# Shift columns, context-first attention units and a joined last phase in a two-block fp32 kernel

## The chip, the core and the metric

One core of one Trainium2 chip runs the whole program. The metric is the device time of one execution in microseconds (us); shown are medians of several runs. The engines are TensorE (PE, with its weight loads apart as PEld), VectorE (DVE), ScalarE (ACT), GpSimd (POOL) and SyncE (SP), which issues the DMAs. TensorE's clock has two levels, 2.4 and 1.2 GHz; the profile gives the granted one as a share, so 1.00 is the first and 0.50 the second.

## What is computed

Two blocks over 512 tokens of 1024 channels, all in fp32:

```
first block, twice (l = 0, 1), mod = ada(c):
  h += 0.5*gate * swiglu(norm(h)*(1+scale) + shift)      # FFN, d_ff 2816
  h += gate * mixer(modulate(norm(h)))                   # sparse attention + gated MLP
  h += 0.5*gate * swiglu(modulate(norm(h)))              # FFN
h = norm(h)*final_g
second block (latents h, 256 context tokens ctx):
  layer 0: h, ctx += gate * norm(pool_mixer(modulate(norm(.))))
           h, ctx += gate * norm(sq_relu_mlp(modulate(norm(.))))   # d_ff 4096
  layer 1: q, k, v = qkv of modulate(norm(h)) and modulate(norm(ctx)); norm, rope
           h += gate * norm(attend(q, k_all, v_all) @ w_o)
           h += gate * norm(sq_relu_mlp(modulate(norm(h))))
```

## The kernel before

Channels lie on partitions, tokens along the free axis. Each fp32 operand is split into a high and a low part, and each product is three matmuls of 512 columns (`mm3`, lines 114 to 116: weight-high by data-high, weight-high by data-low, weight-low by data-high). Weights come as 512 KB chunks on SP's queue into `raw`; ACT writes the high part (L98), DVE or POOL the low one (L100). A framework orders the instructions of each engine by its own model of readiness, with program order as priority, and places the semaphores; a step written later can so be issued earlier, except where an order is kept by hand (the transposes).

The stages, in us of the profiled execution: FFN (0,0) 0 to 410; mixer 0 to 840; FFN (0,1) to 1205; FFN (1,0) to 1560; mixer 1 to 1985; FFN (1,1) to 2355; the pooled mixer and the first MLP, with the context's MLP woven in, to 2920; QKV to 3075; attention to 3184; `w_o` to 3228; the last MLP to 3628.

**The start of a stage.** `Pre` (L237) lets a stage's first products begin before the normalisation of its input is known: `chunk` (L252) scales a finished chunk of h by the gain into `r`, the first products run on `r` (L284, L298, L324, L358), and the token factor and the shift are put in afterwards (`take`, L394). The shift then needs one column per product, weights times shift vector: `shift_products` (L209 to L223) is eight POOL instructions on one weight chunk, and a 128x1 matmul sums them (L310). Where the columns were made ahead, `shift_steps` (L225) did it in the filler of an earlier FFN: a DMA of the 512 KB chunk into `adaw`, the eight POOL instructions, the matmul L233 and a copy. `issue` (L305) starts a stage with its first two products side by side and, if no columns were made ahead, has POOL work and column matmuls in it; `first_two`, `both` and `last_two` do the same with another grouping, and `slow` puts the squares' sums (L150) on DVE where the first four are otherwise on POOL. Before the change the mixers and the first MLP had their columns ahead; FFNs (0,1), (1,0), (1,1) and the last MLP had not.

**The filler.** `ffn` (L495) draws steps of a generator between its product units; a pair such as (3, 2) gives the steps per unit. The steps compute the modulation vectors on DVE (L423, 1024 elements by a row, with an accumulator read behind it). What is left is drained at L554.

**The first MLP** (L1356 to L1460). After `pre.normed`, h is multiplied by `b1s`, eight DVE instructions (L1448, L1449); only then the main loop begins, in which `weave` mixes steps of the MLP (`mlp_steps`, L1319) with steps of the context's MLP at the rates of `WEAVE` (L38). The first four hidden products' results lie in PSUM until `take` (L401, `px`) has read them; the context's products (`nc`) want a PSUM bank too.

**QKV** (L1467 to L1633). Units 0 to 3 are queries, 4 keys, 5 values; each has two weight chunks, and 4 and 5 take two context tiles beside the four latent ones. `tok_proj` (L1555) does a unit's products (L1567 to L1569, 256 columns), its low weight parts on POOL; `heads` (L1572) norms and rotates on ACT and DVE into tiles `hx` of a pool of seven; `transposed` (L1606) is TensorE transposes (L1616) and a split. The loop at L1622 runs the units in the order 0, 1, 4, 2, 3, 5, with the transposes of a unit after the products of the next. Units 0 and 1 start from products made earlier (`first_tiles`).

**w_o and the last MLP** (L1675 to L1714) are two scopes with their own pools: `w_o`'s eight products, its norm, the residual (L1107, L1108) with `Pre.chunk`; then `issue` and the MLP.

Of the kernel before, what the change touches and what calls it, by code (L numbers as in the profile page):

```python
# [19 lines left out]
S = 512  # L20
# [17 lines left out]
WEAVE = (2, 3, 3, 1.65, 3)  # L38
# [13 lines left out]
def build(tc, d, stop=99):  # L52
# [412 lines left out]

    class Phase:
# [28 lines left out]
    def ffn(l, s, mods, fill, pre, tail, nf=(2, 2), start=None):  # L495

        with ExitStack() as st:
# [7 lines left out]
            def wsrc(n):  # L505
                return d["ffn_in"][l, s, n // 2, :, (n % 2) * 1024:(n % 2) * 1024 + 1024]
# [547 lines left out]
    for l in range(L):  # L1054
# [14 lines left out]
        box, tail = pre_tail(modsB, norm_g(l, 2))  # L1069
# [233 lines left out]
    def mlp_src(i, q):  # L1303
# [5 lines left out]
        ada2(p, 1, [ml1, mc1]), ctx_steps(ph), shift_steps(p, ml[:, 24:32], [mlp_src(0, q) for q in range(4)], mlp_cols)),  # L1309
        pre, ft, (3, 3))  # L1310
# [45 lines left out]
    with ExitStack() as st:  # L1356
# [74 lines left out]
        b1s = ph.hid_p.tile([128, S], F32, name="b1s", tag="hid0")  # L1431
# [18 lines left out]
        if stop <= 7:  # L1450
            st.close()
            nst.close()
            return finish_debug()

        ry = Rms(S, tmp)
# [11 lines left out]
    with ExitStack() as st:  # L1467
# [3 lines left out]
        with ExitStack() as ist:  # L1471
# [67 lines left out]
            bcl = bcast(r, S)  # L1539
            nh = [[rtile() for _ in range(2)] for _ in range(8)]  # L1540
            nhi, nlo = (lambda k: nh[k][0]), (lambda k: nh[k][1])
            modulate(h, bcl, gs, sh, S, tmp, nhi, nlo)
# [12 lines left out]
            def tok_proj(src, ctx):  # L1555

                tiles = ([(nch, ncl, 0), (nch, ncl, 1)] if ctx else []) + [(nhi, nlo, i) for i in range(4)]
                pss = [psum() for _ in range(len(tiles) // 2)]
                for k4 in range(2):
                    hi, lo = wget(src[:, k4 * 1024:(k4 + 1) * 1024], eng=G)  # L1560
                    for kk in range(4):
                        k = k4 * 4 + kk
                        w0, w1 = hi[:, kk * 256:(kk + 1) * 256], lo[:, kk * 256:(kk + 1) * 256]
                        for t, (xh, xl, i) in enumerate(tiles):
                            sl = slice(i * 128, (i + 1) * 128)
                            o = pss[t // 2][:, (t % 2) * 256:(t % 2) * 256 + 256]
                            T.matmul(o, xh(k)[:, sl], w0, start=k == 0 and t % 2 == 0, stop=False)  # L1567
                            T.matmul(o, xh(k)[:, sl], w1, start=False, stop=False)
# [278 lines left out]
```

## Time and profile before

| what | value |
|---|---|
| time, median of 3 runs | 3621.99 us (3616.54 to 3625.24) |
| the profiled execution's own time | 3629.45 us |
| its span in the profile | 3627.7 us |
| granted clock, mean | 0.979 |
| PE busy / PEld busy | 3472.6 us (96%) / 2861.7 us (79%) |
| DVE / ACT / POOL busy | 2299.2 (63%) / 1462.9 (40%) / 476.0 us (13%) |
| HBM read and written | 458.63 MB, 126 GB/s over the span |

The profiled execution lies 7.46 us above the median. Busy shares are means over stages that differ: in FFN (1,0) DVE is busy 259.1 of 355 us, in the last MLP with its start 190.3 of 399.7. What an edit in one stage is worth is read from the idle times of PE in that stage and from the granted clock there. A wait is put down to the one that ended last; square brackets at a line's end give the engine's idle time before it and what released it.

### The profile page before, as it was taken

How to read it: one execution, taken by the hardware profiler on the slowest of the kernel's cores; microseconds unless marked ns; L12 is line 12 of the kernel's file. 1: busy time of each engine (PE TensorE's matmuls, PEld its weight loads, DVE VectorE, ACT ScalarE, POOL GpSimd, SP SyncE). 2: the span in 40 equal slices, each digit the busy share in tenths (PEclk: the TensorE clock that was granted, in tenths of full speed). 3: DMA queues.
4: the chain of work that ended last, by engine and by line, in shares of the span. 5: the costliest groups of instructions: out<-in, count | busy, mean ns of one | idle time of the engine just before them, and what ended most of it. 6: DMA issues, size and time to landing. Idle time of an engine off the chain costs nothing.

```text
span 3627.7 us, 44600 instructions
## 1 busy us (share of the span) xinstructions
PE 3472.6 (96%) x16924; PEld 2861.7 (79%) x16924; DVE 2299.2 (63%) x3715; ACT 1462.9 (40%) x2487; POOL 476.0 (13%) x470
## 2 busy tenths in 40 slices
PE   7999999999999999999999999979999988989998
PEld 5788886788878888887688888868888877767886
DVE  8863677458753996378636966675445578654434
ACT  4222475433223422257624224654433435634232
POOL 4020113021000303022104020210000021130000
PEclk9999999999999999999999999989999999999999
DMA  6862221236862475231123763314444421013332
GB/s 237 287 235 92 95 77 48 69 103 240 292 210 91 156 244 171 88 109 51 44 88 133 248 234 99 108 56 134 128 130 127 133 66 59 1 47 99 97 96 70
DMA packets 140985, 461.55 MB, mean 127 GB/s; under 512 B 16869, under 2 KB 19297, under 8 KB 140641
## 3 DMA queue, kind: packets, MB, share of 16 engines
q1 hardware_dynamic: 140768, 458.69, 38.9%
q8 instruction: 133, 2.18, 0.2%
q14 instruction: 84, 0.68, 0.1%
HBM read 456.53 MB, written 2.10 MB: 126 GB/s over the span
## 4 chain that ended last, share of the span: by engine, by line
PE 63%; DVE 7%; ACT 2%; issue 1%; POOL 1%; DMA 1%; SPq 0%; DVEq 0%; ACTq 0%; POOLq 0%
PE mm L114 18%; PE mm L116 18%; PE mm L115 18%; DVE nt L200 1%; DVE wlo L100 1%; PE mm L324 1%; PE aux L1665 1%; PE aux L886 1%; DVE h L1108 0%; DVE n L206 0%; PE o L854 0%; ACT whi L98 0%; DVE ssum L150 0%; POOL shp L215 0%; PE o L115 0%
## 5 line engine op out<-in xcount | busy, mean ns | idle before, releaser
L98 ACT ACTIVATE whi<-raw 128x1024 fp32r<-128x1024 f32 (+2 forms) x636 | 619.3, 976 | 1469.1 <-PE mm L115 1075.0
L100 DVE TENSOR_TENSOR wlo<-raw,whi 128x1024 fp32r<-128x1024 f32 (+3 forms) x605 | 694.7, 1150 | 506.9 <-ACT whi L98 499.0
L114 PE MATMUL mm<-n,whi 128*128 128x512 f32 x2096 | 831.5, 397 | 14.2 <-ACT nt L202 9.2
L116 PE MATMUL mm<-n,wlo 128*128 128x512 f32 x2096 | 824.6, 394 | 4.3 <-DVE wlo L100 4.1
L115 PE MATMUL mm<-n,whi 128*128 128x512 f32 x2096 | 822.8, 393 | 0.4 <-DVE n L206 0.2
L114 PEld LDWEIGHTS mm<-n,whi 128*128 128x128 f32 x2096 | 395.8, 189 | 98.4 <-issue 11.3
L116 PEld LDWEIGHTS mm<-n,wlo 128*128 128x128 f32 x2096 | 395.3, 189 | 95.7 <-DVE wlo L100 7.3
L115 PEld LDWEIGHTS mm<-n,whi 128*128 128x128 f32 x2096 | 395.7, 189 | 85.2 <-DVE n L206 0.9
L423 DVE SCALAR_TENSOR_TENSOR junk<-adaw,crow 128x1024 f32<-128x1024 f32 x288 | 353.3, 1227 | 76.7 <-DMA adaw<-adaT 59.3
L114 PE MATMUL mm<-r,whi 128*128 128x512 f32 x976 | 385.5, 396 | 4.6 <-ACT r L254 3.1
L116 PE MATMUL mm<-r,wlo 128*128 128x512 f32 x976 | 385.1, 395 | 0.1
L115 PE MATMUL mm<-r,whi 128*128 128x512 f32 x976 | 382.3, 392 | 0.2 <-DVE r L108 0.2
L114 PEld LDWEIGHTS mm<-r,whi 128*128 128x128 f32 x976 | 183.6, 188 | 44.4 <-ACT r L254 4.0
L116 PEld LDWEIGHTS mm<-r,wlo 128*128 128x128 f32 x976 | 183.9, 188 | 43.0 <-DVE wlo L100 0.8
L115 PEld LDWEIGHTS mm<-r,whi 128*128 128x128 f32 x976 | 184.0, 189 | 41.6 <-DVE r L108 0.5
L114 PE MATMUL mm<-hid,whi 128*128 128x512 f32 x448 | 176.7, 394 | 0.0
L116 PE MATMUL mm<-hid,wlo 128*128 128x512 f32 x448 | 175.7, 392 | 0.0
L115 PE MATMUL mm<-hid,whi 128*128 128x512 f32 x448 | 174.7, 390 | 0.0
L563 DVE SCALAR_TENSOR_TENSOR h<-mm,hg,h 128x512 f32<-128x512 f32 x96 | 71.9, 749 | 118.5 <-PE mm L116 118.2
L150 POOL TENSOR_TENSOR ssum<-ssum,sq 128x512 f32<-128x512 f32 x27 | 40.6, 1504 | 778.2 <-ACT sq L149 778.2
L545 DVE TENSOR_TENSOR hd<-mm,sil 128x512 f32<-128x512 f32 x79 | 54.4, 688 | 116.0 <-PE mm L116 115.7
L108 DVE TENSOR_TENSOR ptl<-aux,pth 128x512 fp32r<-128x512 f32 x144 | 94.7, 684 | 43.8 <-ACT pth L107 43.2
(500 smaller groups left out, 5808.3 us busy)
## 6 DMA issues: line engine op xcount, KB each, us to landing
adaw<-adaT SPq DMA_DIRECT2D x240, 512.0 KB, 4.8
raw<-ffn_in SPq DMA_DIRECT2D x170, 512.0 KB, 4.6
raw<-mlp_in SPq DMA_DIRECT2D x96, 512.0 KB, 3.8
raw<-ffn_out SPq DMA_DIRECT2D x64, 512.0 KB, 4.3
raw<-mlp_out SPq DMA_DIRECT2D x64, 512.0 KB, 3.8
raw<-mlp_out SPq DMA_DIRECT2D x64, 256.0 KB, 2.9
raw<-ffn_out SPq DMA_DIRECT2D x32, 384.0 KB, 3.1
raw<-mix_zb SPq DMA_DIRECT2D x16, 512.0 KB, 3.6
```

The lines of the kernel that those rows point to most:

```text
L98: A.activation(hi[:, :F], raw, AF.Copy)
L100: (eng or cur["lo"]).tensor_tensor(lo[:, :F], raw, hi[:, :F], op=OP.subtract)
L108: (eng or V).tensor_tensor(lo, src, hi, op=OP.subtract)
L114: T.matmul(ps, lh, rh, start=start, stop=False)
L115: T.matmul(ps, lh, rl, start=False, stop=False)
L116: T.matmul(ps, ll, rh, start=False, stop=stop)
L150: self.last = (eng or V).tensor_tensor(self.acc, self.acc, sq, op=OP.add)
L200: V.scalar_tensor_tensor(t, src[:, k], gs[:, k:k + 1], bc, op0=OP.mult, op1=OP.mult)
L324: T.matmul(self.pss[n], w[:, sl], x, start=k + e == 0, stop=k == DC - 1 and e == 2)
L423: V.scalar_tensor_tensor(junk, w, 1.0, cs[v], op0=OP.mult, op1=OP.mult, accum_out=mods[v][:, j * 8 + m:j * 8 + m + 1])
L545: V.tensor_tensor(hd, pss[1], sil, op=OP.mult)
L563: V.scalar_tensor_tensor(h[:, m], ps, hg[:, m:m + 1], h[:, m], op0=OP.mult, op1=OP.add)
```

## The change

Four parts.

- **Shift columns.** FFNs (0,1), (1,0) and (1,1) and the last MLP take their shift columns from the filler of an earlier FFN: `shift_steps` runs for 16 more chunks, that is 16 DMAs of 512 KB more, the same POOL instructions in another place, and two filler steps for each. Three FFNs have another pair of rates: (0,1) from (3, 2) to (3, 3), (1,0) from (2, 3) to (3, 2), (1,1) from (3, 3) to (3, 4).
- **First MLP.** Two hidden products are taken before `pre.normed`; the eight multiplications by `b1s` are handed out from the seventh step of the first part on, one after each; `b1s` lies in another pool; the rate of context steps behind `last_two` is 4 and not 3.
- **QKV.** The keys' unit comes first, its context tiles before the normalised latents are made (`mid`); a unit's two weight chunks are fetched together; the transposes of a unit stand behind the products of a later unit.
- **w_o and the last MLP** share one phase and its pools; `first_two`, `both` and `last_two` with `slow` take the place of `issue`.

```diff
-WEAVE = (2, 3, 3, 1.65, 3)
+WEAVE = (2, 3, 3, 1.65, 4)
...
+    def ffn_src(l, s, n):
+        return d["ffn_in"][l, s, n // 2, :, (n % 2) * 1024:(n % 2) * 1024 + 1024]
...
+        ahead2 = lambda p, l=l, m=modsB, b=cols: shift_steps(p, m[:, 0:8], [ffn_src(l, 1, n) for n in range(4)], b[:, 4:8])
         if l == 0:
-            fill = lambda p, ph: chain(ada1(p, 0, 1, modsA), ada1(p, 0, 2, modsB), ahead(p))
+            fill = lambda p, ph: chain(ada1(p, 0, 1, modsA), ada1(p, 0, 2, modsB), ahead(p), ahead2(p))
             ffn(l, 0, mods0, fill, None, tail, (3, 2), start)
         else:
...
-            ffn(l, 0, mods0, lambda p, ph: chain(ada2(p, 0, ml), ahead(p)), pre, tail, (2, 3))
+            ffn(l, 0, mods0, lambda p, ph: chain(ada2(p, 0, ml), ahead(p), ahead2(p)), pre, tail, (3, 2))
...
-        box, tail = pre_tail(modsB, norm_g(l, 2))
+        box, tail = pre_tail(modsB, norm_g(l, 2), cols=cols[:, 4:8])
...
-            fill = lambda p, ph: chain(ada1(p, 1, 0, mods0), ada1(p, 1, 1, m1), ada1(p, 1, 2, m2))
-            box, tail = pre_tail(mods0, norm_g(1, 0))
-            ffn(0, 1, modsB, fill, pre, tail, (3, 2))
+            cols = shift_cols()
+            fill = lambda p, ph: chain(ada1(p, 1, 0, mods0), ada1(p, 1, 1, m1), ada1(p, 1, 2, m2),
+                                       shift_steps(p, mods0[:, 0:8], [ffn_src(1, 0, n) for n in range(4)], cols))
+            box, tail = pre_tail(mods0, norm_g(1, 0), cols=cols)
+            ffn(0, 1, modsB, fill, pre, tail, (3, 3))
...
-        ada2(p, 1, [ml1, mc1]), ctx_steps(ph), shift_steps(p, ml[:, 24:32], [mlp_src(0, q) for q in range(4)], mlp_cols)),
-        pre, ft, (3, 3))
+        ada2(p, 1, [ml1, mc1]), ctx_steps(ph), shift_steps(p, ml[:, 24:32], [mlp_src(0, q) for q in range(4)], mlp_cols),
+        shift_steps(p, ml1[:, 24:32], [mlp_src(1, q) for q in range(4)], mlp_cols[:, 4:8])), pre, ft, (3, 4))
...
-        b1s = ph.hid_p.tile([128, S], F32, name="b1s", tag="hid0")
+        b1s = cur["cx"].tile([128, S], F32, name="b1s", tag="ssum512b")
...
         ph.n_tiles()
+        ry = Rms(S, tmp)
+        parts = [mlp_steps(0, p, 8, S, ph.nhi, ph.nlo, lambda m: yl[:, m], ph, lambda q: ph.hid(q not in (0, 4)), ry, 4,
+                           pre if p == 0 else None) for p in range(4)]
+        run_steps(parts[0], 2)
         pre.normed(ph.nhi, ph.nlo)
-        for k in range(DC):
-            V.tensor_tensor(h[:, k], h[:, k], b1s, op=OP.mult)
...
+        def factor(gen):
+            for i, _ in enumerate(gen):
+                if i > 5:
+                    V.tensor_tensor(h[:, i - 6], h[:, i - 6], b1s, op=OP.mult)
+                yield
+
+        parts[0] = factor(parts[0])
         ctx_lo[0] = V
-        for p in range(4):
-            weave(mlp_steps(0, p, 8, S, ph.nhi, ph.nlo, lambda m: yl[:, m], ph, lambda q: ph.hid(q not in (0, 4)), ry, 4,
-                            pre if p == 0 else None), WEAVE[3])
+        for p in parts:
+            weave(p, WEAVE[3])
...
-            def tok_proj(src, ctx):
+            def tok_proj(src, ctx, mid=None):
...
+                pss = [psum() for _ in range(3 if ctx else 2)]
+                ws = [wget(src[:, k4 * 1024:(k4 + 1) * 1024], eng=G) for k4 in range(2)]
...
+                if ctx:
+                    for k in range(DC):
+                        for i in range(2):
+                            products(i, nch, ncl, i, k)
+                if mid is not None:
+                    mid()
+                for k in range(DC):
+                    for i in range(4):
+                        products(i + 2 * ctx, nhi, nlo, i, k)
...
-            late = None
-            for u in (0, 1, 4, 2, 3, 5):
-                own = first_tiles(u) if u < 2 else None
-                pss = [x[:, 0:256] for x in own] if own else tok_proj(d["qkv"][u], u > 3)
-                if late is not None:
-                    transposed(*late)
...
+            own = first_tiles(0)
+            pk = tok_proj(d["qkv"][4], True, normed)
+            transposed(heads(views(own), 0, tabs[0], own), 0, queries(0))
+            own = first_tiles(1)
+            q1 = heads(views(own), 0, tabs[0], own)
+            p2 = tok_proj(d["qkv"][2], False)
+            transposed(q1, 0, queries(1))
+            k = heads(pk, 2, tabs[1])
+            p3 = tok_proj(d["qkv"][3], False)
+            transposed(k, 2, lambda e, a: kT[e][:, a])
+            q2 = heads(p2, 0, tabs[0])
+            pss = tok_proj(d["qkv"][5], True)
+            transposed(q2, 0, queries(2))
+            transposed(heads(p3, 0, tabs[0]), 0, queries(3))
...
-        pre.issue([(lambda q=q: wload(d["mlp_in"][1, q // 2, :, (q % 2) * 1024:(q % 2) * 1024 + 1024])) for q in range(4)])
...
+        pre = Pre(*modcols(ml1, pc("g_mlp_pre_2", 8), 3, 4), tmp, mlp_cols[:, 4:8], slow=True)
+        pre.first_two([lambda q=q: wload(mlp_src(1, q)) for q in range(2)])
+        bc = ry.finish()
+
+        def chunk(k, x):
+            pre.chunk(k, x)
+            pre.both(k)
+
+        post(h, lambda k: yo[:, k], bc, colprod(ml1[:, 16:24], pc("g_mix_post_2", 8)), S, tmp, chunk)
+        pre.last_two([lambda q=q: wload(mlp_src(1, q)) for q in range(2, 4)])
         pre.normed(ph.nhi, ph.nlo, (3, 6))
```

## Rows read from the trace of the kernel before

**Rows 1.** The page's part 1: busy time, share of the span, instructions, by engine.
```profile
PE 3472.6 (96%) x16924; PEld 2861.7 (79%) x16924; DVE 2299.2 (63%) x3715; ACT 1462.9 (40%) x2487; POOL 476.0 (13%) x470
```

**Rows 2.** PE's waits over the span: us in total, times, longest.
```profile
PE aux L184 <- DVE rs_y L133: 14.4, 7, 3.1
PE mm L324 <- ACT r L254: 7.7, 6, 2.9
...
PE mm L114 <- DVE px L401: 7.5, 2, 7.2
PE aux L1616 <- DVE hx L1602: 5.1, 4, 1.9
...
PE aux L310 <- POOL shu L222: 3.3, 3, 1.5
...
PE aux L1616 <- DVE hx L1592: 2.9, 1, 2.9
```

**Rows 3.** Windows: stretch, length, busy PE, PEld, DVE, ACT, POOL, clock, DMA share, GB/s.
```profile
1991.30:1994.70 3.40, 3.40 (x9) 2.63 (x10) 3.40 (x8) 2.08 (x3) 1.26 (x1) 0.50 0.00 0
3443.00:3483.00 40.00, 40.00 (x176) 32.78 (x175) 19.45 (x23) 15.11 (x21) 0.00 (x0) 1.00 0.31 92
1240.00:1280.00 40.00, 40.00 (x176) 32.85 (x175) 39.29 (x64) 12.28 (x16) 0.00 (x0) 1.00 0.73 243
880.00:920.00 40.00, 38.65 (x168) 31.13 (x167) 28.91 (x47) 11.61 (x14) 0.00 (x0) 1.00 0.84 300
```

**Rows 4.** Timeline of PE in FFN (0,0), around one column of the filler.
```profile
333.33 0.39 PE L116 MATMUL mm<-n,wlo 128*128 128x512 f32 x1
333.56 0.28 PE L233 MATMUL aux<-ones,shu 128*128 128x1 f32 x2
...
334.25 0.39 PE L116 MATMUL mm<-n,wlo 128*128 128x512 f32 x1
```

**Rows 5.** Groups of L423, 1240 to 1400: ns min/median/max, first and last start.
```profile
L423 DVE SCALAR_TENSOR_TENSOR junk<-adaw,crow x89: 1210/1219/1510, 1239.0 to 1398.3; 128x1024 f32<-128x1024 f32 x89
```

**Rows 6.** Timeline of the first MLP, behind its norm.
```profile
2442.84 0.68 DVE L1449 TENSOR_TENSOR h<-h,b1s 128x512 f32<-128x512 f32 x1
...
2444.77 4.29 DVE L1449 TENSOR_TENSOR h<-h,b1s 128x512 f32<-128x512 f32 x7
...
2449.81 0.55 PE L114 MATMUL mm<-nc,whi 128*128 128x256 f32 x1 [7.24 <-DVE px L401]
```

**Rows 7.** Windows of the first MLP's start and of QKV.
```profile
2436.00:2456.00 20.00, 10.71 (x59) 9.74 (x59) 19.71 (x28) 10.44 (x17) 1.73 (x1) 0.66 0.25 77
2998.00:3077.00 79.00, 68.81 (x518) 66.00 (x516) 68.55 (x187) 46.44 (x166) 13.46 (x5) 0.94 0.16 50
```

**Rows 8.** Timeline of DVE and POOL in QKV.
```profile
3013.08 0.17 DVE L133 SCALAR_TENSOR_TENSOR rs_y<-rs_b,rs_y 128x8 f32<-128x8 f32 x1
...
3013.23 2.40 POOL L100 TENSOR_TENSOR wlo<-raw,whi 128x1024 fp32r<-128x1024 f32 x1 [17.88 <-ACT whi L98]
...
3013.28 2.36 DVE L131 TENSOR_TENSOR rs_a<-rs_y 128x8 f32<-128x8 f32 x1
```

**Rows 9.** Group of L100 on POOL, 2985 to 3080.
```profile
L100 POOL TENSOR_TENSOR wlo<-raw,whi x7: 2374/2395/3406, 2990.6 to 3050.9; 128x1024 fp32r<-128x1024 f32 x7
```

**Rows 10.** Timeline of ACT, DVE and POOL between w_o and the last MLP.
```profile
3246.70 0.72 ACT L254 ACTIVATE r<-h,gs 128x512 fp32r<-128x512 f32 x1 [2.01 <-DVE h L1108]
...
3248.09 1.29 POOL L150 TENSOR_TENSOR ssum<-ssum,sq 128x512 f32<-128x512 f32 x1 [1.97 <-ACT sq L149]
3248.13 1.80 DVE L1108 TENSOR_TENSOR h<-pt,h 128x512 f32<-128x512 f32 x1
...
3250.02 0.72 ACT L254 ACTIVATE r<-h,gs 128x512 fp32r<-128x512 f32 x1 [2.07 <-DVE h L1108]
```

**Rows 11.** Timeline of ACT at the first MLP's start.
```profile
2408.22 0.72 ACT L254 ACTIVATE r<-h,gs 128x512 fp32r<-128x512 f32 x1 [1.69 <-DVE h L1108]
...
2410.96 0.72 ACT L254 ACTIVATE r<-h,gs 128x512 fp32r<-128x512 f32 x1 [1.50 <-DVE h L1108]
```

More of the change, by code (lines that the diff above doesn't have):

```diff
@@ L505, in wsrc @@
             def wsrc(n):
[L506 removed]
+                return ffn_src(l, s, n)
             def product(n):
@@ L1553, in first_tiles, with products @@
                 return out
-            def tok_proj(src, ctx):
[L1557 to L1568, printed above, removed]
-                            T.matmul(o, xl(k)[:, sl], w0, start=False, stop=k == 7 and t % 2 == 1)
-                return [pss[t // 2][:, (t % 2) * 256:(t % 2) * 256 + 256] for t in range(len(tiles))]
+            def tok_proj(src, ctx, mid=None):
+                pss = [psum() for _ in range(3 if ctx else 2)]
+                ws = [wget(src[:, k4 * 1024:(k4 + 1) * 1024], eng=G) for k4 in range(2)]
+                def products(t, xh, xl, i, k):
+                    w0, w1 = (x[:, (k % 4) * 256:(k % 4) * 256 + 256] for x in ws[k // 4])
+                    sl = slice(i * 128, (i + 1) * 128)
+                    o = pss[t // 2][:, (t % 2) * 256:(t % 2) * 256 + 256]
+                    T.matmul(o, xh(k)[:, sl], w0, start=k == 0 and t % 2 == 0, stop=False)
+                    T.matmul(o, xh(k)[:, sl], w1, start=False, stop=False)
+                    T.matmul(o, xl(k)[:, sl], w0, start=False, stop=k == 7 and t % 2 == 1)
+                if ctx:
[7 more added lines that the diff above has]
+                        products(i + 2 * ctx, nhi, nlo, i, k)
+                return [pss[t // 2][:, (t % 2) * 256:(t % 2) * 256 + 256] for t in range(2 * len(pss))]
             def heads(pss, nctx, tab, own=None):
@@ L1619, in transposed, with queries, views @@
                         t0 += w
[L1621 to L1630 removed]
+            def queries(u):
+                return lambda e, a: qT[e][:, 2 * u + a]
+            def views(own):
+                return [x[:, 0:256] for x in own]
+            own = first_tiles(0)
[12 more added lines that the diff above has]
+            transposed(heads(p3, 0, tabs[0]), 0, queries(3))
             for t, ps in enumerate(pss):
@@ L1674, in build @@
                         split(oh[4 * g + q][:, sl], ol[4 * g + q][:, sl], bc[:, q * 128:(q + 1) * 128], G)
-        box, tail = pre_tail(ml1, pc("g_mlp_pre_2", 8), 3, 4)
-        with ExitStack() as ist:
-            cur["mm"] = pool(ist, "mm", 6, space=PSUM)
-            t_p = pool(ist, "ltmp", 8)
-            def tmp(name):
-                return t_p.tile([128, S], F32, name=name, tag="t2")
-            yl = yq_p.tile([128, DC, S], F32, name="yo", tag="qT0")
-            ry = Rms(S, tmp)
-            for m in range(8):
-                hi, lo = wget(d["w_o"][m // 2, :, (m % 2) * 1024:(m % 2) * 1024 + 1024])
-                ps = psum()
-                dense(ps, hi, lo, 8, lambda k: oh[k], lambda k: ol[k])
-                A.activation(yl[:, m], ps, AF.Copy)
-                ry.add(yl[:, m])
-            bc = ry.finish()
-            post(h, lambda k: yl[:, k], bc, colprod(ml1[:, 16:24], pc("g_mix_post_2", 8)), S, tmp, tail(tmp))
-    yst.close()
     nst.close()
-    if stop <= 9:
-        return finish_debug()
     with ExitStack() as st:
@@ L1703, in build @@
         y = yp.tile([128, DC, S], F32, name="yl")
-        pre = box[0]
-        pre.tmp = tmp
-        pre.issue([(lambda q=q: wload(d["mlp_in"][1, q // 2, :, (q % 2) * 1024:(q % 2) * 1024 + 1024])) for q in range(4)])
+        yo = yq_p.tile([128, DC, S], F32, name="yo", tag="qT0")
+        ry = Rms(S, tmp)
+        for m in range(8):
+            hi, lo = wget(d["w_o"][m // 2, :, (m % 2) * 1024:(m % 2) * 1024 + 1024])
+            ps = psum()
+            dense(ps, hi, lo, 8, lambda k: oh[k], lambda k: ol[k])
+            A.activation(yo[:, m], ps, AF.Copy)
+            ry.add(yo[:, m])
+        pre = Pre(*modcols(ml1, pc("g_mlp_pre_2", 8), 3, 4), tmp, mlp_cols[:, 4:8], slow=True)
[6 more added lines that the diff above has]
+        pre.last_two([lambda q=q: wload(mlp_src(1, q)) for q in range(2, 4)])
         pre.normed(ph.nhi, ph.nlo, (3, 6))
+        if stop <= 9:
+            st.close()
+            yst.close()
+            return finish_debug()
         ry = Rms(S, tmp)
@@ L1714, in build @@
              lambda k, x: SY.dma_start(d["outT"][:, k], x))
+    yst.close()
     top.close()
```

17 lines of the change are left out of this document (5 added, 12 removed).

## The prediction

> **What bounds the kernel now.** The first view is the page's part 1: TensorE is busy 96% of the span, and no other engine is near it [rows 1]. So a change that takes no product away can only win back TensorE's idle time, 155 us of the span, and what the lower clock costs. The second view is the list of PE's waits over the span [rows 2]: they are many and short, the longest of those shown is 7.2 us, and each belongs to a place where a stage begins or its order turns. The third are windows [rows 3]. Where all is well, 40.00 us hold 176 products of 512 columns, 0.2275 us each; this pitch prices all that follows, and one of 256 columns is taken at half, 0.114. At some seams where PE had just been idle a stretch runs at clock 0.50, the 1.2 GHz level; there a product takes twice its pitch, so such a stretch with PE busy throughout costs half its length. The reader is to see that the four parts of the change aim at four kinds of seam, and that at two of them DVE is nearly as full as PE.
>
> The sum is made on the profiled execution, 3629.45 us (span 3627.7 and 1.75 around it). It lies 7.46 above the median of the three runs, 3621.99; the gain is taken off the median.
>
> **Shift columns.** Removed at three FFN starts: the wait of the last column matmuls for POOL, 3.3 us in three places, longest 1.5 [rows 2]. Behind the one of FFN (1,1), 3.4 us run at clock 0.50 with PE busy throughout [rows 3], which costs 1.7. Together 5.0. The column matmuls themselves only move: in the filler a column costs (334.25 - 333.33) - 3 x 0.2275 = 0.24 us of PE [rows 4], two instructions of the shape that the starts hold now, so the twelve columns of the FFNs (2.9 us) and the four of the last MLP (1.0) are taken in one place and paid in another: nothing. The 128 POOL instructions move too. Sixteen DMAs of 512 KB are new on SP's queue, between the weights of the products that run beside the filler. At 300 GB/s, the rate of the fullest FFN [rows 3], 8.4 MB are 28 us of the DMA engines. In FFN (0,1), (0.84 of the engines, PE 38.65 of 40.00 [rows 3]) the new four come behind the last step of the modulation, where that load has ended. I take nothing; the bound is the 1.35 us lost in that window, once more.
>
> The rates must make room for eight more steps in each of four FFNs. In FFN (1,0) DVE is busy 39.29 of 40.00, with PE at 40.00 [rows 3]; most of it is the filler's instruction of 1.22 us, 89 in 160 us [rows 5]. That is 89/160 x 10.92 = 6.1 for a unit of 48 products, three steps of two instructions, although the code asks for two steps in some units and three in others: DVE takes what it can now. So the pair (3, 2) asks for the pace that is run already. If it does press the unit's own evictions behind a step, that is half an instruction or so, 0.6 us, in at most eight units: 5 us as the bound, 0.5 as the value, nearest to PE's 40.00 of 40.00. Of FFN (0,0)'s longer chain two steps are left to its drain, where nobody waits for their columns for a whole mixer. Sum: 4.5 us (-2 to 6.5).
>
> **First MLP.** Behind the norm PE idles 7.24 us until `px` has emptied a bank; DVE in that time runs eight multiplications by `b1s`, 0.68 the first and 4.29 the other seven [rows 6]. The change takes two hidden products ahead of the norm, so two banks are free before it, and the multiplications go behind steps of the down projection: 5.0 us of DVE among 8 x 24 x 0.2275 = 44 us of products and the context's beside them; that cover gone, they would cost 5.0. The two `px`, of a multiplication's shape, now stand ahead of the normalised tiles, 1.4 us, and DVE, at 19.71 of 20 [rows 7], has no room to hide them: 7.24 - 1.4 = 5.8. The mean clock of these 20 us is 0.66, so 13.6 are at the half level; PE is busy 10.71, at least 4.3 of them there, which costs 2.2 or more. I count 1.2 of it: 7 us. Ends: 3, if the context's products that fill the gap are then missing behind it; 11, if the whole stretch goes.
>
> **QKV.** At the transposes PE waits 5.1 us in four places and 2.9 in one for `hx` [rows 2]. The mean clock of 0.94 over 79 us [rows 7] says 9.5 us at the half level, worth 4.7. With the transposes two units back all that would be 12.7 us. But DVE is busy 68.55 of the 79 [rows 7], so no order of TensorE's work brings more than the 10.45 us that DVE is idle, unless DVE's own work shrinks. Some of it is waiting: a 128x8 step of the rsqrt takes 0.17, and 2.36 where it starts beside POOL's low part of 2.40 [rows 8]. There are seven such low parts [rows 9], up to 7 x 2.2 = 15 us of DVE's busy time; they stay, and where they fall is chance. I take half of DVE's idle time, 5 us. Bounds: 10 above, -3 below, for one more pause like the longest for `rs_y`, 3.1 [rows 2]. That pause itself, ahead of the latents' norm, only moves: the context's 24 products of the second weight chunk (24 x 0.114 = 2.7 us) can fill it now, and are then missing behind it, where PE waits for the first normalised tile.
>
> The Trainium skill (SBUF — State Buffer, section "Who interferes with whom") says that a VectorE instruction with two SBUF inputs and a GpSimd instruction that reads SBUF contend for shared ports, and that who starts first holds them for its whole length. The 2.36 beside 2.40 agrees. By that rule the moved shifts could go on holding VectorE up in the fillers, against this change; no row here shows it, and the sum would lose no more than the bound of the rates above.
>
> **w_o and the last MLP.** Grouping the products otherwise gains nothing: `issue` has its first two interleaved now. The chain of sum, rsqrt and residual keeps its waits, among them 2.9 for `r` [rows 2]. What changes is the chunks' pace: 3.32 us from one `r` to the next, while POOL adds the squares and DVE's residual beside it takes 1.80 [rows 10], against 2.74 at the first MLP's start, where DVE adds them itself [rows 11]. Four chunks, 0.58 x 3.5 = 2.0 us; the four sums that DVE gets are in the 2.74 already. I take 1.5 (-1, if the later wait for the normalised tiles eats it and a sum comes late; 4, if the pauses between the chunks' products close as well).
>
> **Sum.** 4.5 + 7 + 5 + 1.5 = 18. Own time 3629.45 - 18 = 3611.5; from the median 3604.
>
> **The rivals.** *QKV and the last MLP bring nothing*, since TensorE's work is ordered by readiness anyhow and DVE's order stays: 4.5 + 7 = 11.5, so 3610.5. For it: at the transposes TensorE waits for DVE and not DVE for TensorE [rows 2].
>
> *Gaps only move*: DVE, at 39.29 of 40, 19.71 of 20 and 68.55 of 79 [rows 3, 7], is late next at each seam, and the lower clock stays; the columns' 5.0 remain: 3617. For it: DVE has 0.3 us of slack in the 20 in which the first MLP's 7.24 lie. Against it: the eight multiplications leave just that window.
>
> *Slower, QKV in series*: `hx` has seven tiles, `heads` of the keys needs six, and the four of unit 1 are held until its transposes, which now stand behind the 96 products of unit 2, 96 x 0.114 = 10.9 us. If DVE is through with unit 1 long before these products, it has nothing to do until they end; the same comes again for unit 2 behind the keys' transposes. Twice some 10.5 us of DVE's time, on a stage that DVE fills to 87%: 21 longer, with the other parts' 13 gained 3622 + 21 - 13 = 3630. It decides from the point where the transposes end over 7 us later than DVE finishes the unit before. Against it: in the trace of before the transposes wait for DVE, by 1.9 us and more [rows 2].
>
> *The change doesn't do what it says*: had a filler too few slots, the columns would come at its drain and the next start would wait for them as now: 4.5 less, 3608.5, inside the range and counted with the second case.
>
> **How the numbers follow.** Forecast 3604 with a chance of 0.53; QKV and last MLP nothing (or the columns late) 0.22; gaps only move 0.16; slower 0.09. About 0.2% (7.2 us) is what a measurement of this kernel can tell from no change. Faster by more than that is below 3614.8: the first case and nearly all of the second: 0.73. Within, up to 3629.2: the rest of the second and the third, 0.18. Slower: 0.09. The range: the low ends of the gains add up to -2 + 3 - 3 - 1 = -3, the high ends to 31.5, so 3590.5 to 3625; since not all fall on one side together it is cut to 3620 above, and the slower rival is left out: 3590 to 3620.
>
> **What would show it.** Right: no wait for `shu` behind an FFN's start and clock 1.00 there; no wait for `px` of 7 us; the QKV stretch shorter by about 5 us, with DVE's busy share up from 0.87 to 0.93; `r` to `r` at 2.75 us behind `w_o`. Wrong: pauses of PE in FFN (1,0) for evictions or weights while the filler runs; DVE idle for 5 us and more at a time ahead of `hx`; the half-clock stretch in the first MLP as long as before.

## The result and the profile after

The changed kernel takes 3662.28 us (median of 4 runs, 3655.31 to 3664.46), the kernel before 3623.61 in the same comparison: a ratio of 1.0107, 95% interval 1.0087 to 1.0127. It is 38.7 us slower; 3604 was forecast. The profiled execution took 3664.46 us, with a span of 3662.5.

Where the time went is read stage by stage. The sum matmuls L163 of a large norm mark a stage's end in the timeline of PE. Nine of these marks are used, the first stage counts from the span's start, and 17.8 us follow the last mark in both kernels. The stages are so cut a little later than the rounded bounds given with the kernel before. Each length is that of one profiled execution:

| stage (us) | before | after | difference | forecast |
|---|---|---|---|---|
| FFN (0,0) | 418.9 | 427.8 | +8.8 | 0 |
| FFN (0,1) | 372.6 | 388.7 | +16.1 | in the -4.5 |
| FFN (1,0) | 368.1 | 366.3 | -1.8 | in the -4.5 |
| FFN (1,1), with the pooled mixer's start | 425.7 | 438.0 | +12.3 | in the -4.5 |
| first MLP | 555.8 | 554.2 | -1.6 | -7 |
| QKV, attention, w_o | 278.3 | 279.8 | +1.5 | -5 |
| last MLP | 378.9 | 378.7 | -0.2 | -1.5 |
| the two mixers | 811.6 | 811.3 | -0.3 | 0 |

So the shift columns cost 35 us where 4.5 were to be gained, and the other three parts together brought nothing. PE's busy time has hardly moved (3472.6 us [rows 1] to 3476.7), so this is idle time and lower clock. The page's part 1:

```profile
PE 3476.7 (95%) x16924; PEld 2867.2 (78%) x16924; DVE 2282.1 (62%) x3729; ACT 1461.5 (40%) x2487; POOL 458.0 (13%) x468
```

PE's longest new waits over the span (us in total, times, longest):

```profile
PE mm L114 <- ACT r L107: 17.1, 2, 14.9
...
PE mm L114 <- ACT nc L107: 11.4, 4, 5.3
PE mm L114 <- ACT whi L98: 9.9, 4, 4.5
...
PE mm L115 <- POOL n L108: 4.1, 1, 4.1
```

Two windows, with the columns of [rows 3]:

```profile
1062.00:1080.00 18.00, 3.41 (x7) 2.42 (x8) 4.91 (x6) 5.12 (x6) 5.71 (x9) 0.63 0.57 202
2213.00:2245.00 32.00, 23.31 (x99) 19.52 (x100) 27.28 (x72) 15.46 (x33) 0.84 (x12) 0.79 0.28 91
```

The waits that were to go are gone at the FFNs' starts and in the first MLP: `shu` at L310 and `px` at L401 [rows 2] no longer stand in the list. New ones have come: 14.9 us for `r` in FFN (0,1), with 18 us in which PE is busy 3.41 at a mean clock of 0.63; four waits for `nc` in FFN (1,1); 4.1 us for a normalised tile from GpSimd in the last MLP.

**The 14.9 us.** Stretches of the timeline of SP, ACT and PE (start, us, instruction; the bracket is the idle time before it):

```profile
1050.63 0.33 SPq L229 DMA_DIRECT2D adaw<-ffn_in  x1
1051.01 0.42 SPq L93 DMA_DIRECT2D raw<-ffn_out  x1
1051.48 0.42 SPq L412 DMA_DIRECT2D crow<-c  x1
1067.47 0.33 SPq L412 DMA_DIRECT2D crow<-c_ctx  x1
...
1068.37 0.38 SPq L93 DMA_DIRECT2D raw<-ffn_out  x1
...
1071.74 1.06 ACT L413 ACTIVATE crow<-crow 128x1024 f32<-128x1024 f32 x1 [13.22 <-DMA crow<-c_ctx]
1072.70 1.04 ACT L98 ACTIVATE whi<-raw 128x1024 fp32r<-128x1024 f32 x1
...
1076.32 0.79 PE L114 MATMUL mm<-r,whi 128*128 128x512 f32 x1 [14.90 <-ACT r L107]
```

The timeline of POOL, the ends of two columns:

```profile
1057.36 0.46 POOL L222 TENSOR_TENSOR shu<-shp 128x128 f32<-128x128 f32 x1
...
1062.86 0.45 POOL L222 TENSOR_TENSOR shu<-shp 128x128 f32<-128x128 f32 x1
```

Read the first from the top. SP issues nothing between 1051.9 and 1067.5. It stands at the second load of the next filler, `crow<-c_ctx`, whose buffer lies where the shift columns' still do, and GpSimd takes 5.5 us for each column (from one L222 to the next). ACT's order has the activation of this load (L413) ahead of the next high parts of the weights: it waits 13.22 us for it, and only then come `whi` (L98) and `sil` (L547). The two chunks issued at 1045.73 and 1051.01 had landed 5.2 us after their issue, so here it is ACT that holds them, and not their own place in SP's queue. PE comes last. PE's list names only the end of this chain, ACT. SP's own list of waits names its beginning:

```profile
SPq L229 <- POOL shp L215: 94.4, 16, 8.5
...
SPq L412 <- POOL shp L215: 12.5, 1, 12.5
```

The same list of the kernel before, which the prediction did not read, showed that SP waits for GpSimd at all: three times, for columns made ahead.

```profile
SPq L229 <- POOL shp L215: 18.3, 3, 7.3
```

Such a wait is not yet a loss. Of the 94.4 us after, these lie in FFN (1,0) (1225 to 1590), where PE waits for nothing and the stage is 1.8 us shorter than before:

```profile
SPq L229 <- POOL shp L215: 29.3, 5, 7.1
```

In FFN (0,0), where 31.8 us lie, one of them does reach PE, by the other way: a weight chunk stands behind two shift loads in SP's queue, ACT waits for it, and PE idles 4.54 us at 267.5.

```profile
253.99 7.18 SPq L229 DMA_DIRECT2D adaw<-ffn_in  x2
261.22 0.42 SPq L93 DMA_DIRECT2D raw<-ffn_in  x1
...
266.35 1.06 ACT L98 ACTIVATE whi<-raw 128x1024 fp32r<-128x1024 f32 x1 [10.23 <-DMA raw<-ffn_in]
```

### The profile page after: what moved, and what is told of

The parts are those of the page before. It is cut to its first block, busy times and chain, and to the rows that moved or that the text cites. A ratio compares the mean times of both kernels' runs of the same rounds, so it can differ in the third digit from the quotient of the medians.

```text
span 3662.5 us, 44646 instructions
## 1 busy us (share of the span) xinstructions
PE 3476.7 (95%) x16924; PEld 2867.2 (78%) x16924; DVE 2282.1 (62%) x3729; ACT 1461.5 (40%) x2487; POOL 458.0 (13%) x468
## 4 chain that ended last, share of the span: by engine, by line
PE 75%; DVE 12%; DMA 5%; issue 3%; ACT 3%; POOL 2%; SPq 0%; DVEq 0%; ACTq 0%; POOLq 0%
PE mm L114 21%; PE mm L116 20%; PE mm L115 20%; DMA adaw<-adaT 4%; PE mm L324 2%; DVE junk L423 2%; DVE wlo L100 1%; PE aux L889 1%; DVE nt L200 1%; PE o L857 1%; PE o L858 1%; DVE n L206 1%; PE s L324 1%; PE s L818 1%; POOL shp L215 1%
## 5 line engine op out<-in xcount | busy, mean ns | idle before, releaser
L98 ACT ACTIVATE whi<-raw 128x1024 fp32r<-128x1024 f32 (+2 forms) x636 | 619.7, 976 | 1487.8 <-PE mm L115 1046.9
L100 DVE TENSOR_TENSOR wlo<-raw,whi 128x1024 fp32r<-128x1024 f32 (+3 forms) x604 | 695.3, 1153 | 564.5 <-ACT whi L98 557.0
L114 PE MATMUL mm<-r,whi 128*128 128x512 f32 x992 | 394.2, 400 | 23.8 <-ACT r L107 17.1
L423 DVE SCALAR_TENSOR_TENSOR junk<-adaw,crow 128x1024 f32<-128x1024 f32 x288 | 354.1, 1229 | 76.2 <-DMA adaw<-adaT 57.7
L116 PE MATMUL mm<-r,wlo 128*128 128x512 f32 x992 | 393.0, 396 | 0.0
L115 PE MATMUL mm<-r,whi 128*128 128x512 f32 x992 | 391.3, 394 | 0.9 <-DVE r L108 0.8
L114 PEld LDWEIGHTS mm<-r,whi 128*128 128x128 f32 x992 | 188.1, 190 | 66.0 <-ACT r L107 17.9
L115 PEld LDWEIGHTS mm<-r,whi 128*128 128x128 f32 x992 | 188.5, 190 | 44.7 <-DVE r L108 2.1
L215 POOL TENSOR_TENSOR shp<-adaw,m 128x256 f32<-128x256 f32 x80 | 59.6, 751 | 522.0 <-DMA adaw<-mix_ck 329.8
```

Source lines behind the costliest of these rows:

```text
L98: A.activation(hi[:, :F], raw, AF.Copy)
L100: (eng or cur["lo"]).tensor_tensor(lo[:, :F], raw, hi[:, :F], op=OP.subtract)
L114: T.matmul(ps, lh, rh, start=start, stop=False)
L115: T.matmul(ps, lh, rl, start=False, stop=False)
L116: T.matmul(ps, ll, rh, start=False, stop=stop)
L215: G.tensor_tensor(o.rearrange("p (k m) -> p k m", k=n), raw[:, k * 128:(k + n) * 128].rearrange("p (k m) -> p k m", k=n), sh[:, k:k + n].r ...
```

## The experiments

All kernels below "after" but the last two are the changed one with one or two edits. Lengths of the stages touched, read as above:

| kernel | median us | FFN (0,0) | (0,1) | (1,0) | (1,1) | first MLP | QKV to w_o | last MLP |
|---|---|---|---|---|---|---|---|---|
| before | 3623.6 | 418.9 | 372.6 | 368.1 | 425.7 | 555.8 | 278.3 | 378.9 |
| after | 3662.3 | 427.8 | 388.7 | 366.3 | 438.0 | 554.2 | 279.8 | 378.7 |
| shift loads from GpSimd's queue | 3656.6 | 425.1 | 388.7 | 366.2 | 438.0 | 553.3 | 280.6 | 374.9 |
| no columns ahead for FFNs | 3639.0 | 420.6 | 373.9 | 367.9 | 441.5 | 554.1 | 280.3 | 374.0 |
| rates (3, 3) in (1,1) | 3652.1 | 429.0 | 387.2 | 366.3 | 433.0 | 553.7 | 280.3 | 374.8 |
| two seams | 3654.8 | 431.1 | 390.8 | 366.2 | 439.4 | 553.9 | 280.4 | 372.0 |
| columns earlier in the fillers | 3647.0 | 426.1 | 382.9 | 366.2 | 434.9 | 553.3 | 280.1 | 374.8 |
| the same, GpSimd's queue | 3644.7 | 419.1 | 390.6 | 366.2 | 435.0 | 554.4 | 280.6 | 374.8 |
| old QKV | 3653.5 | 426.0 | 391.9 | 366.2 | 439.5 | 553.7 | 277.2 | 374.0 |
| own buffer in (0,1) | 3644.4 | 428.7 | 379.2 | 366.2 | 438.1 | 553.7 | 280.3 | 374.0 |
| loads only | 3640.5 | 429.8 | 371.4 | 366.3 | 439.2 | 553.3 | 280.6 | 374.8 |
| before with the new QKV | 3625.7 | 420.7 | 372.3 | 367.9 | 424.4 | 555.7 | 278.6 | 378.9 |
| parts worth keeping | 3615.7 | 418.5 | 370.4 | 369.3 | 422.2 | 553.8 | 276.4 | 376.0 |

A stage whose text is the same differs from kernel to kernel by some us: (0,0) between 426.0 and 431.1 in six of them with SP's queue, (0,1) between 387.2 and 391.9, the mixers between 400.1 and 409.2 each. The later stages vary less where their text is the same: the last MLP between 374.0 and 374.9 in eight kernels, QKV between 279.8 and 280.6. Differences below a stage's own spread are not read here.

**Who issues the loads.**

```diff
-            SY.dma_start(w, src)
+            G.dma_start(w, src)
             r = shift_products(sh, w)
```

> The sixteen new loads and the older ones of the shift steps are issued by GpSimd and no longer by SP; nothing else is changed from the changed kernel. Theory 1 (SP's queue is in order: a shift load that waits for a buffer which GpSimd still reads holds the weight chunks behind it): the pauses of 4.5 us at 267 and of 14.9 us at 1076 go, FFN (0,0) is about 7 us shorter and FFN (0,1) about 15, 3662 - 22 = 3640. Theory 2 (the 8.4 MB more load the DMA engines, whoever issues them): the pauses stay, 3660. The pauses of FFN (1,1) at 2215 and 2240 stay by both.

Neither theory came out whole. In FFN (0,0) the pause of 4.5 us goes. In (0,1) it is 13.9 now: SP issues no shift load any more, and still waits for GpSimd, at the next filler's second load (SP's waits, 1036 to 1076):

```profile
SPq L412 <- POOL shp L215: 11.8, 1, 11.8
```

So it is not the shift load that stands in the way, but whoever wants its buffer next.

**The part as a whole.**

```diff
-            fill = lambda p, ph: chain(ada1(p, 0, 1, modsA), ada1(p, 0, 2, modsB), ahead(p), ahead2(p))
+            fill = lambda p, ph: chain(ada1(p, 0, 1, modsA), ada1(p, 0, 2, modsB), ahead(p))
...
-            ffn(0, 1, modsB, fill, pre, tail, (3, 3))
+            ffn(0, 1, modsB, fill, pre, tail, (3, 2))
```

(and in the same way in FFNs (0,1) and (1,0), without their four columns)

> The three FFN starts make their shift columns themselves again, with the old rates in (0,1) and (1,0); the last MLP keeps its columns from the filler of FFN (1,1), and all the rest is as changed. Theory 1 and theory 2 alike: FFN (0,0) and (0,1) go back to their old lengths, 8.8 and 16.1 us shorter, the three starts cost their 5 again, of which 1.8 show in FFN (1,0): 3662 - 22 = 3640. If the rates and not the columns were the cause, the same; so this run gives the price of that part as a whole and e1 tells what it consists of. A price under 10 us would say that the loss lies in FFN (1,1) and behind it.

3639.0, as both had it, 23 us below the change by the medians. Stage by stage the columns of the three FFN starts cost 17 of it: FFN (0,0) and (0,1) are 7.2 and 14.8 shorter, (1,0) and (1,1), which make their own columns again, 1.6 and 3.5 longer. The rest is in the mixers and the last MLP, which this edit does not touch, so that the number came out so near is in part luck. What stays, 15 us over the kernel before, is nearly all in FFN (1,1).

**FFN (1,1): the rate.**

```diff
-        shift_steps(p, ml1[:, 24:32], ...)), pre, ft, (3, 4))
+        shift_steps(p, ml1[:, 24:32], ...)), pre, ft, (3, 3))
```

> FFN (1,1) runs with the rates (3, 3) and not (3, 4); its eight more filler steps stay. Theory (the higher rate draws the context's pooling steps to a place where PE's order has no products to cover the chain from the context's norm to its first product): the four waits for nc, 11.4 us, and the two stretches at the lower clock go, FFN (1,1) 12 us shorter, 3650. Rival (the four more columns push the context's steps or hold the weights): the waits stay, 3662.

The four waits for `nc` go, as the theory said; but only 5 us of the stage come back, not 12. (The median of 3652.1 lies near the forecast of 3650 by luck: 3.9 us of it are in the last MLP, whose text is the same.) In the timeline of PE after, the two longest are these:

```profile
2215.64 0.80 PE L114 MATMUL mm<-nc,whi 128*128 128x256 f32 x2 [5.33 <-ACT nc L107]
...
2240.45 0.50 PE L114 MATMUL mm<-nc,whi 128*128 128x256 f32 x2 [4.21 <-ACT nc L107]
```

With the old rate the same view has these:

```profile
2333.31 0.38 PE L233 MATMUL aux<-ones,shu 128*128 128x1 f32 x2 [2.65 <-POOL shu L222]
...
2339.38 0.59 PE L233 MATMUL aux<-ones,shu 128*128 128x1 f32 x2 [2.48 <-POOL shu L222]
```

At three steps the filler does not end in time: the last columns are made in its drain, where PE waits for GpSimd at their matmuls, and 10 us there run at clock 0.50. At four it ends in time, and the context's pooling steps come to where PE's order holds too few products to cover them. Eight more steps have a price either way: 7 us or 12.

**Two seams.** In the last MLP and in QKV:

```diff
-        pre.normed(ph.nhi, ph.nlo, (3, 6))
+        pre.normed(ph.nhi, ph.nlo)
...
-            pk = tok_proj(d["qkv"][4], True, normed)
+            normed()
+            pk = tok_proj(d["qkv"][4], True)
```

> Two places in separate stages. In the last MLP no normalised tile is made on GpSimd (before: tiles 3 and 6). Theory (GpSimd's low part of tile 3 takes 5.3 us beside DVE's two-input instructions, where it took 1.8 before): the wait of 4.05 us for that tile goes, the last MLP is 3 to 4 us shorter. Rival (DVE is full there, the tile is late on it as well): 0 to 1 us. In QKV the latents' norm stands ahead of the keys' products again: theory (the context's products first only move the wait, and the chain ahead of the norm is late for another reason, the context's norm between the steps of the rsqrt): the stretch to the first transposes of the factor changes by less than 1 us; rival: it is 3.4 us shorter. Together 3658, or 3655 with the rival of QKV.

The last MLP is 372.0, 6.7 shorter than in the kernel after. But eight other kernels of the same text show 374.0 to 374.9, so only 2 to 3 us belong to the edit; the other 4 are one event of the profiled execution of after. The timelines of POOL and DVE after:

```profile
3305.65 7.51 POOL L108 TENSOR_TENSOR n<-nt,n 128x512 fp32r<-128x512 f32 x2 [83.19 <-ACT n L107]
...
3305.75 2.07 DVE L200 SCALAR_TENSOR_TENSOR nt<-h,gs,bcs 128x512 f32<-128x512 f32 x3
...
3309.73 0.68 DVE L401 TENSOR_TENSOR px<-mm,bcs 128x512 f32<-128x512 f32 x1
```

The two instructions of POOL apart (ns min/median/max; the first is the long one):

```profile
L108 POOL TENSOR_TENSOR n<-nt,n x2: 2253/3770/5287, 3305.7 to 3310.9; 128x512 fp32r<-128x512 f32 x2
```

The same in the kernel with the loads from GpSimd's queue, where its first tile is alone:

```profile
3303.78 1.31 POOL L108 TENSOR_TENSOR n<-nt,n 128x512 fp32r<-128x512 f32 x1 [84.08 <-ACT n L107]
...
3303.87 3.10 DVE L200 SCALAR_TENSOR_TENSOR nt<-h,gs,bcs 128x512 f32<-128x512 f32 x3
```

The two tiles took 7.5 us together after, the first 5.3 of it; the first took 1.3 in the other, and in seven more of these kernels. In the other it is DVE that is drawn out: its three instructions beside GpSimd's take 3.10 us, and 2.07 after. After, GpSimd's first ends 1.2 us behind the start of `px`, the first DVE instruction there with an input in PSUM. The Trainium skill (SBUF — State Buffer, section "Who interferes with whom") has it that the issue order decides which of VectorE and GpSimd blocks; in each kernel one of the two is drawn out, which agrees, but GpSimd's record starts 0.1 us ahead of DVE's in both, so the rows do not show the order itself. QKV is 280.4: the context's products first bring nothing, as expected.

**Columns earlier.**

```diff
-            fill = lambda p, ph: chain(ada1(p, 1, 0, mods0), ada1(p, 1, 1, m1), ada1(p, 1, 2, m2),
-                                       shift_steps(p, mods0[:, 0:8], ..., cols))
+            fill = lambda p, ph: chain(ada1(p, 1, 0, mods0),
+                                       shift_steps(p, mods0[:, 0:8], ..., cols),
+                                       ada1(p, 1, 1, m1), ada1(p, 1, 2, m2))
...
-        ada2(p, 1, [ml1, mc1]), ctx_steps(ph), shift_steps(...), shift_steps(...)), pre, ft, (3, 4))
+        ada2(p, 1, [ml1, mc1]), shift_steps(...), shift_steps(...), ctx_steps(ph)), pre, ft, (3, 4))
```

> Only the order of two fillers differs from the changed kernel, all loads on SP: in FFN (0,1) the four shift columns stand behind the first modulation vector (which they need) and two more of DVE's groups stand behind them; in FFN (1,1) the eight columns stand ahead of the context's pooling steps, rates (3, 4) kept. Theory, as the first runs left it: what stops SP in FFN (0,1) is the next filler's first load, of crow, which waits 12 us for GpSimd to be through with the columns at the filler's end; with DVE's groups behind them the pause of 14.9 us and its half-clock stretch go, FFN (0,1) from 388.7 to 374, and the context's steps come as late as before: no waits for nc, FFN (1,1) from 438 to 427. Together 3662 - 25 = 3637. Rival (GpSimd and DVE slow each other wherever the columns run): a pause of 5 us and more moves to where the columns are now, FFN (0,1) at 380 and more.

> As the run before, and the shift loads issued by GpSimd. Theory: SP then never waits for GpSimd in the fillers, FFN (0,0) as in the first run of this kind 425 (427.8 without), FFN (0,1) 372 to 374, the rest as the run before: 3634. If SP's wait for shift loads alone cost nothing, the same as the run before.

The pause of 14.9 goes, and of the 16.1 us that the stage had lost only 5.8 go with it: seven waits for `wlo`, 9.2 us, come in its place, 382.9 us, nearer to the rival's number. The rival's reason is not seen: the filler's instruction of 1.22 us [rows 5] keeps its length (850 to 1100, ns min/median/max), though only two of the 72 run beside an instruction of GpSimd. SP's list for FFN (0,1) says what is:

```profile
L423 DVE SCALAR_TENSOR_TENSOR junk<-adaw,crow x72: 1208/1224/1227, 855.3 to 1053.0; 128x1024 f32<-128x1024 f32 x72
...
SPq L421 <- POOL shp L215: 17.8, 3, 6.5
...
SPq L229 <- POOL shp L215: 4.7, 1, 4.7
```

The modulation's loads (L421) take turns in the same three buffers as the shift's. With GpSimd issuing the shift loads it is still 15.6 us in three waits, and the stage 390.6. In FFN (1,1) one wait for `nc` of 4.6 us stays in either; the stage is 434.9, and the forecast of 427 was wrong by 8.

**A buffer of its own.** The four columns of FFN (0,1), early as before:

```diff
+            if own:
+                w = p.tile([128, 1024], F32, name="shw", tag="shw")
+                G.dma_start(w, src)
+            else:
                 w = p.tile([128, 1024], F32, name="adaw", tag="adaw", bufs=3)
                 SY.dma_start(w, src)
```

> The changed kernel with FFN (0,1)'s four shift columns behind its first modulation vector, in a buffer of their own (one) and loaded from GpSimd's queue; everything else as changed. Theory (what costs there is that the shift steps share three buffers with the modulation's loads on SP, so that SP waits for GpSimd and the weight chunks behind it come late; the same order with the shared buffers gave 382.9 and 390.6): FFN (0,1) at 373 to 376, no pause above 2 us but the old ones, SP with no wait for GpSimd's shift instructions; in all 3662 - 14 = 3648. Rival (GpSimd's work beside DVE's is what slows the filler, or TensorE waits at the column matmuls for a slower GpSimd): 380 and more, with pauses at L233 or DVE's instructions drawn out.

In this stage SP no longer waits for GpSimd, and its length is 379.2: nearer to the theory, but 3 us above its range. One pause of 8.2 us is left. ACT stands at a late `crow` with `whi` behind it, as in the change, but what SP waited for ahead of this load is DVE and not GpSimd. ACT's timeline, at the first load of the second modulation:

```profile
924.48 1.06 ACT L417 ACTIVATE crow<-crow 128x1024 f32<-128x1024 f32 x1 [10.95 <-DMA crow<-c]
925.44 1.04 ACT L98 ACTIVATE whi<-raw 128x1024 fp32r<-128x1024 f32 x1
```

**Loads without GpSimd's work.** The run that separates GpSimd's work from the traffic:

```diff
-            r = shift_products(sh, w)
+            r = ident if loads else shift_products(sh, w)
```

> The changed kernel, in which the sixteen new steps load their weight chunk, but GpSimd's eight instructions on it are left out; the column matmul reads the identity in their place, so the shift of four stages is not the reference's. Steps, rates, order and all DMAs stay. Theory (the price is SP waiting for GpSimd to give back a buffer): FFN (0,0) 419 to 421, FFN (0,1) 373 to 376 with no pause of 14 us; FFN (1,1) keeps its waits for nc (they come from the steps' order), 436 to 438; 3662 - 22 = 3640. Rival (the 8.4 MB on the DMA engines are the price): FFN (0,0) 425 and more, FFN (0,1) 385 and more, 3660.

FFN (0,1) is 371.4: its four new loads are there, at the same rates, and nothing is lost. So it is neither the bytes nor the rate (3, 3), but what GpSimd does between the load and the next one. By itself this run does not part the time for which GpSimd keeps the buffers from its work beside DVE; that it is the buffers is read from SP's waits, from the filler's length in the run with the columns earlier, and from the run with a buffer of its own, in which GpSimd's work stayed and SP's wait for it went. In FFN (0,0) this run missed: 429.8, with a pause of 5.3 us. There the mixer's four columns, which are of the kernel before, keep their GpSimd work; the new loads stand behind them in SP's queue and a weight chunk behind those. With the loads on GpSimd's queue this pause is gone in both kernels; their 425.1 and 419.1 for this stage do not tell what is left of its price. That the whole came out at the forecast 3640 is so in part luck: the miss of 10 us there is made up in the main by the mixers and the last MLP, whose text is that of the change.

**QKV.** The old code in the changed kernel, and the new code in the kernel before (the diff is the one shown, backward and forward):

> The changed kernel with the old QKV: units in the order 0, 1, 4, 2, 3, 5, transposes one unit back, norm first, weight chunks fetched one by one. Theory (that part loses 1.5 to 2 us net: what it gains at the transposes it loses ahead of the latents' norm): 3660, the stage from the first pause of its first norm to w_o's norm 278.3, not 279.8 to 280.6. Rival (the loss ahead of the norm comes from the first MLP's changed order and not from QKV's): 281 and more, 3664.

> The kernel before with the new QKV alone (units' order, transposes later, both weight chunks at once). Theory from the run with the old QKV in the changed kernel (277.2 against 279.8 to 280.6): the stage from the norm ahead of QKV to w_o's norm 281 and not 278.3, the whole 3 us slower than before, 3627. Rival (the part only loses behind the changed first MLP): 278 and less, 3623.

277.2 against 279.8 to 280.6, so the part costs some 3 us behind the changed first MLP (one execution each); alone its stage is 0.3 longer (278.6), as the rival had it, and not the forecast 281. But the whole is then 0.10% slower (ratio 1.0010, 1.0001 to 1.0019, that is 0.4 to 6.9 us), as the theory had it. So that the loss belongs to the two parts together is what the one profiled execution says, and is not shown.

**What is worth keeping.** On the kernel before: the columns of FFN (1,1) made in FFN (1,0), the changed first MLP, and in the last MLP no GpSimd work in the norm:

```diff
-            ffn(l, 0, mods0, lambda p, ph: chain(ada2(p, 0, ml), ahead(p)), pre, tail, (2, 3))
+            ffn(l, 0, mods0, lambda p, ph: chain(ada2(p, 0, ml), ahead(p), ahead2(p)), pre, tail, (3, 2))
...
+            chunk = tail(tmp)
+            box[0].slow = True
...
-        pre.normed(ph.nhi, ph.nlo, (3, 6))
+        pre.normed(ph.nhi, ph.nlo)
```

> The kernel before with what the runs left worth having: FFN (1,1)'s four columns made in FFN (1,0), rates (3, 2) there; the changed first MLP; in the last MLP all squares and all normalised tiles on DVE and ACT, none on GpSimd, in the old scopes. Sum from the stages of the runs so far: FFN (1,0) 0 (its own start keeps its wait, in the changed kernel it was 1.8 shorter without), FFN (1,1) -3.2 (its 1.5 of wait and 1.7 at the lower clock), first MLP -2, last MLP -2 to -5: 3624 - 8 = 3616. Rival (the order that the framework finds elsewhere shifts with it, as the mixers' 400 to 408 us show): 3620 to 3628.

3615.7 us, a ratio of 0.9974 to the kernel before (0.9965 to 0.9984): 8 us faster than before and 47 faster than the change. FFN (1,1) gives 3.4, the first MLP 2.0, the last 2.9, FFN (1,0) takes 1.1. The rest was not edited: the mixers' 8 us and FFN (0,1)'s 2 may be an execution's luck. QKV's 1.9 has company, since the old QKV behind the changed first MLP took 277.2 in the run above too.

## Why the prediction was wrong

**Shift columns: the step that failed.** The prediction priced the sixteen loads by their bytes ("I take nothing", 1.4 us as the bound) and let the GpSimd instructions "move too". As work both were sized rightly where it was tried: the loads alone cost FFN (0,1) nothing. Missing was that buffers join the two. A column holds one for GpSimd's 5.5 us, the next load into that place waits at the head of SP's queue, and all loads behind it wait too: the weights of the products in FFN (0,0) (4.5 us of PE), and in FFN (0,1) a load for which ACT, with the weights' high parts behind it in its own order, stands as long (14.9 us). The price of the three FFNs' columns is 17 us by the stages, 23 by the medians. The step that asks what is queued behind a waiting instruction was made for PE and never for SP and ACT. In FFN (1,0) SP waited as long and PE lost nothing; why there was slack there is not shown.

**The rates.** FFN (1,0) behaved as forecast: (3, 2) asks for the pace that DVE ran already, 366.3 us, 1.8 shorter. Pauses of PE there, which the prediction named as a sign of being wrong, did not come. The other end was not looked at: FFN (1,1) has no room for eight steps more without moving the context's steps, 7 to 12 us. What is left to the drain was counted in FFN (0,0), where nobody waits; for (1,1) neither the drain at the old rate, where PE waits, nor what the rate (3, 4) brings forward was asked.

**The starts themselves** were right: the wait for `shu` and the half-clock stretch behind it are gone (the granted clock is 1.00 from 2008 to 2028, at FFN (1,1)'s start), and FFN (1,1) shows it in the best kernel, -3.4 for the 3.2 of 1.5 and 1.7. The prediction's "twice its pitch" at clock 0.50 is a little much: products of 512 columns start 0.42 us apart there (2335.43 to 2336.28 in the run with the old rate), 1.9 times 0.2275.

**First MLP: mechanism right, size wrong.** The wait for `px` went. 7.24 - 1.4 supposed that only the two `px` stand ahead of the tiles. The two products bring their squares and splits too; ACT and DVE run these among the normalised tiles, and behind them wait the context's weights. The window (columns of [rows 3]) and PE's rows there:

```profile
2476.00:2490.00 14.00, 6.37 (x29) 5.46 (x29) 13.41 (x20) 8.56 (x13) 0.00 (x0) 0.64 0.31 92
...
2478.21 0.39 PE L114 MATMUL mm<-nc,whi 128*128 128x256 f32 x1 [1.78 <-ACT whi L98]
...
2479.16 0.38 PE L114 MATMUL mm<-nc,whi 128*128 128x256 f32 x1 [0.44 <-ACT whi L98]
...
2482.82 0.58 PE L114 MATMUL mm<-nc,whi 128*128 128x256 f32 x1 [3.16 <-ACT whi L98]
...
2485.86 0.58 PE L116 MATMUL mm<-nc,wlo 128*128 128x256 f32 x1 [2.25 <-DVE wlo L100]
```

7.6 us of new waits for 7.2 and 1.9 of old ones: -1.4 to -2.5 in all kernels with the part. The rival "gaps only move", with DVE at 19.71 of 20 [rows 7], was the case here: DVE is busy 13.41 of these 14 us, and the lower clock (0.64) came along.

**QKV: the bound was right and the value not.** Waits for `hx` at the transposes fall from 8.0 us in five [rows 2] to 3.5 in three, but 3.0 for `hx` at a product, 1.9 for `rs_a` and 1.1 for `qT` take their place. DVE, which sets the pace, was to rise to 0.93 of the stretch; it is busy 64.43 us of 78 where it was 68.55 of 79. And the norm ahead of it got later. The window after (columns of [rows 3]):

```profile
3032.00:3110.00 78.00, 64.08 (x497) 62.17 (x496) 64.43 (x189) 43.84 (x164) 12.28 (x5) 0.93 0.18 57
```

PE's timeline at that norm:

```profile
2986.17 1.84 PE L163 MATMUL aux<-ones,ssum 128*128 128x1 f32 x8 [4.36 <-DVE ssum L150]
2992.33 1.08 PE L184 MATMUL aux<-ident,rs_y 128*128 128x128 f32 x4 [4.33 <-DVE rs_y L133]
```

The second was 2.5 us before. The rival "QKV in series" did not occur: no idle time of DVE there is above 2.7 us.

**Last MLP: mechanism right, size too small.** The eight kernels with the same text other than after's own profiled execution give -4.0 to -4.9, at its upper bound and above. `r` follows `r` at 2.81 us behind `w_o`, where 2.75 was forecast, and the pauses between the chunks, which the value of 1.5 left in, did close for the most part: PE's waits for `r` fall from 7.7 us in six to 3.5 in three. In after's own execution the late tile of GpSimd took the gain back.

**The slower rival** was placed in QKV, at 3630, while the loss came through a queue and a rate that no rival spoke of. Its chance of 0.09 was too small for a change that adds sixteen loads to the queue that feeds the engine that bounds the kernel.

**What stays open:** what is left of FFN (0,0)'s 8.8 us once SP no longer waits there; the columns of FFN (0,1) at the filler's end, as in the change, with a buffer of their own, which no run has; the 6.6 us that FFN (0,1) keeps with its own buffer and the columns early; and whether the new QKV's stage costs less without the changed first MLP, where the stage says 0.3 us and the whole 0.4 to 6.9.

## What to carry to other kernels

Before work is moved into a filler, read the list of waits of the queue that issues its loads, not only that of the bound engine: a buffer that a slow engine holds stops every load behind the one that wants it, whatever the bytes are. It costs time where the engine that feeds the bound one then runs dry, so follow the loads behind it to what they feed. Work that is off the critical path should not share buffers, or a queue, with the loads that feed it. And a filler has a length: count its steps against its slots in each stage, and look at what a higher rate brings forward.

## What the runs showed of the hardware that was not expected

The same GpSimd instruction, a low part of 128x512, took 5.3 us in one execution and 1.3 in eight kernels with the same instructions beside it: beside a busy DVE its length is not fixed, and a schedule that waits for it has a tail. Loads of 512 KB issued from GpSimd's queue landed as fast as SP's: medians of 4.5 to 5.0 us by tensor in the first run of that kind, and 4.1 to 4.9 for the same loads on SP's queue after.
